# A planner's prices for transfers and GpSimd, and the order of the last seven products, in a two-layer encoder trunk

## The chip, the cores and the metric

The program runs on one core of one Trainium2 chip. The metric is the time of one execution on the device in microseconds; the median of several runs counts. The engines of a core run their own instruction queues in order and wait for each other by semaphores: TensorE (PE, matmuls), VectorE (DVE), ScalarE (ACT), GpSimd (POOL) and SyncE (SP, which here only issues transfers).

## The reference

Two layers over 1024 tokens of width 1024. The mixers (a convolution with a recurrence in layer 0, differential attention in layer 1) are not touched by the change; the feed-forward and the normalization behind it are:

```python
def layer_norm(x, g, b):
    mu = jnp.mean(x, axis=-1, keepdims=True)
    var = jnp.mean(jnp.square(x - mu), axis=-1, keepdims=True)
    return (x - mu) * lax.rsqrt(var + LN_EPS) * g + b

def swiglu(x, w_gate, w_up, w_down):
    return (jax.nn.silu(x @ w_gate) * (x @ w_up)) @ w_down

def reference(x, ...):
    for layer in range(DEPTH):
        y = conv_lru_mixer(x, ...) if layer % 2 == 0 else diff_attention_mixer(x, ...)
        x = layer_norm(DN_ALPHA * x + y, mix_ln_g[layer], mix_ln_b[layer])
        x = layer_norm(DN_ALPHA * x + swiglu(x, ffn_w_gate[layer], ffn_w_up[layer], ffn_w_down[layer]),
                       ffn_ln_g[layer], ffn_ln_b[layer])
    return x
```

D_FF is 2816, everything is float32.

## The kernel before

**Numbers and matmuls.** Each operand of a matmul is split into a high part (a cast to fp32r on ScalarE) and a low part (operand minus high part on VectorE): `split`. `three` then issues three matmuls, high by high, high by low and low by high, of 128x512 each.

**Stages.** Layer 0's input part runs from 0 to about 480 us, its feed-forward's gate and up part to 740 us, its down projection to 1000 us. Layer 1 with the attention follows to 1780 us, then its gate and up part to 2045 us and its down projection to the end. The activations of the feed-forward are 22 pages of 128x1024 (4 KB for each partition). 18 of them go out to memory (`a_d`); the last four stay on the chip.

**The down projection** (`ffn_down`) is a 2x2 block product with seven block products, M1 to M7, in place of eight. A block product sums over 11 columns f; for each f, `operands` makes a left operand out of stored activations and a right operand out of `in_down`, and four token tiles of three matmuls each are run on them: 7 x 11 x 12 = 924 matmuls of a layer. `plan` gives for each product what its operands are made of. `(0, 1), (1, 1), S` means that the block of half 1 of page f less the block of half 1 of page f + 11 is taken. A left sum runs on GpSimd. A right sum with A is two transfers: SyncE loads the first half, GpSimd issues a transfer that adds the second onto it in place. A right difference with S is two loads and a subtraction on VectorE. M3 and M4 have no left sum; M2 and M5 have no right sum. The products run in the order M3 M2 M5 M4 M1 M7 M6 and alternate between two sets of four PSUM banks, `al` and `be`. `into` adds a finished product into the residual pages `self.r` on VectorE (r11 and r12 are the left and right halves of token tiles 0 to 3, r21 and r22 those of tiles 4 to 7).

**Buffers.** `halloc` hands out half pages, of which five pages (ten halves) serve as `raws` and for left sums, in turn. `pair` hands out operand pages: first those lent from the transposed input `xt` (`lend`: eight for each token half), then pages of the general pool. `reclaim` ends the lending; before, it does so for both halves ahead of M6.

**The end of the down projection.** After M7 the tiles 0 to 3 are complete, and `done` normalizes them (`layer_norm`: two statistics, their aggregate and two passes of 1024 on VectorE, a power on GpSimd on a single column). M6 follows; its last three columns are run tile by tile, so that tiles 4 to 7 come one after the other, each with its own normalization. `late` loads gains, transposes tiles 0 to 3 for layer 1, or prefetches its weights.

**What sets the order.** All instructions are recorded (`note`) with a price (`price`), and `solve` plans them. It takes the engine whose next instruction can start first, and among the ready ones that with the earliest due time `late`, which is worked back from the order of TensorE. `apply` fixes the order so found for each engine. Prices and latencies of transfers therefore change where every instruction stands, in the whole program.

## Time and profile before

| | us |
|---|---|
| median of three runs | 2331.08 (2328.5 to 2335.04) |
| the profiled execution | 2323.4 |
| its span | 2321.6 |
| TensorE busy in it | 2168.9 |
| VectorE busy | 1862.2 |
| GpSimd busy | 1020.6 |
| ScalarE busy | 998.6 |

Times of the rows below are microseconds from the start of the span, unless they are marked ns. "g" is a page of the general pool, "xt" a page of the transposed input or one lent from it, "SM" the tile of small columns, "PS" PSUM. All instructions carry line L379 (L380 in the changed kernel), since a recorder issues them; tiles and shapes tell them apart. In the views that list waits, the engine behind the arrow ended the idle time.

### The profile page before, as it was taken

How to read it: one execution, taken by the hardware profiler on the slowest of the kernel's cores; microseconds unless marked ns; L12 is line 12 of the kernel's file. 1: busy time of each engine (PE TensorE's matmuls, PEld its weight loads, DVE VectorE, ACT ScalarE, POOL GpSimd, SP SyncE). 2: the span in 40 equal slices, each digit the busy share in tenths (PEclk: the TensorE clock that was granted, in tenths of full speed). 3: DMA queues.
4: the chain of work that ended last, by engine and by line, in shares of the span. 5: the costliest groups of instructions: out<-in, count | busy, mean ns of one | idle time of the engine just before them, and what ended most of it. 6: DMA issues, size and time to landing. Idle time of an engine off the chain costs nothing.

```text
span 2321.6 us, 28973 instructions
## 1 busy us (share of the span) xinstructions
PE 2168.9 (93%) x9856; PEld 1776.4 (77%) x9856; DVE 1862.2 (80%) x2735; ACT 998.6 (43%) x1751; POOL 1020.6 (44%) x798
## 2 busy tenths in 40 slices
PE   9999898899999999899999998979998999999995
PEld 7877676778888788678777776767776888888884
DVE  8988889887776589894788768767878877779888
ACT  6485336233333343332444445544544333334431
POOL 2123211186666455621334324222244776755464
PEclk9999999999999999999999998999999999999998
DMA  8348875464445866756455479575647444475684
GB/s 238 89 128 200 242 220 186 128 217 164 163 154 162 277 168 161 167 177 197 146 142 167 143 230 266 157 193 157 185 126 245 168 149 160 163 236 203 179 180 127
DMA packets 170084, 415.55 MB, mean 179 GB/s; under 512 B 18512, under 2 KB 38736, under 8 KB 169936
## 3 DMA queue, kind: packets, MB, share of 16 engines
q1 hardware_dynamic: 142864, 364.47, 48.3%
q0 software_dynamic: 27072, 49.24, 13.0%
q8 instruction: 78, 1.28, 0.2%
q14 instruction: 70, 0.57, 0.1%
HBM read 313.03 MB, written 85.98 MB: 172 GB/s over the span
## 4 chain that ended last, share of the span: by engine, by line
PE 65%; DMA 15%; DVE 12%; issue 4%; ACT 2%; POOL 2%; SPq 1%; DVEq 0%; ACTq 0%; POOLq 0%
PE PS L379 65%; DVE g L379 7%; DMA g<-in_down 4%; DMA g<-in_up 4%; DVE xt L379 3%; DMA g<-k_d 2%; ACT g L379 2%; DVE SM L379 2%; POOL g L379 1%; DMA g<-x_d 1%; DMA z_d<-g 1%; DMA g<-in_wout 1%; DMA k_d<-g 1%; SPq L379 1%; DMA q_d<-g 0%
## 5 line engine op out<-in xcount | busy, mean ns | idle before, releaser
L379 POOL TENSOR_TENSOR g<-g,g 128x512 f32<-128x512 f32 x390 | 621.2, 1605 | 509.8 <-ACT g L379 245.1
L379 PE MATMUL PS<-g,xt 128*128 128x512 f32 (+1 forms) x2800 | 646.8, 379 | 18.2 <-DVE g L379 11.0
L379 PE MATMUL PS<-xt,g 128*128 128x512 f32 x2428 | 614.1, 401 | 36.0 <-ACT g L379 19.6
L379 PE MATMUL PS<-xt 128*128 128x512 f32 (+1 forms) x2320 | 619.4, 393 | 10.5 <-ACT g L379 4.1
L379 PEld LDWEIGHTS PS<-g,xt 128*128 128x128 f32 x2800 | 516.1, 190 | 125.7 <-DVE g L379 14.3
L379 PEld LDWEIGHTS PS<-xt,g 128*128 128x128 f32 x2428 | 459.2, 192 | 145.2 <-ACT g L379 29.8
L379 DVE TENSOR_TENSOR xt<-g,xt 128x512 fp32r<-128x512 f32 x531 | 501.0, 969 | 76.4 <-ACT xt L379 73.9
L379 ACT CAST xt<-g 128x512 fp32r<-128x512 f32 x531 | 313.7, 619 | 510.6 <-PE PS L379 338.0
L379 DVE TENSOR_TENSOR g<-g,g 128x512 f32<-128x512 f32 (+2 forms) x457 | 444.5, 986 | 104.9 <-ACT g L379 78.6
L379 PEld LDWEIGHTS PS<-xt 128*128 128x128 f32 x2320 | 437.5, 190 | 105.9 <-ACT g L379 6.7
L379 DVE TENSOR_TENSOR g<-PS,g 128x512 f32<-128x512 f32 (+3 forms) x408 | 257.3, 643 | 159.7 <-PE PS L379 93.8
L379 ACT CAST g<-g 128x512 fp32r<-128x512 f32 (+1 forms) x248 | 188.0, 770 | 293.2 <-DVE g L379 73.6
L379 PE MATMUL PS<-g,g 128*128 128x512 f32 (+3 forms) x984 | 257.0, 381 | 31.1 <-DVE g L379 10.9
L379 DVE SCALAR_TENSOR_TENSOR g<-g,SM,g 128x512 f32<-128x512 f32 (+20 forms) x309 | 262.2, 883 | 2.5 <-POOL SM L379 0.5
L379 ACT ACTIVATE g<-PS,SM 128x512 f32<-128x512 f32 (+8 forms) x266 | 179.2, 688 | 136.6 <-PE PS L379 89.7
L379 PEld LDWEIGHTS PS<-g,g 128*128 128x128 f32 x984 | 176.6, 194 | 68.4 <-DVE g L379 13.7
L379 PE MATMUL PS<-xt,xt 128*128 128x512 f32 (+1 forms) x612 | 213.1, 391 | 1.3 <-DVE g L379 1.3
L379 POOL TENSOR_TENSOR g<-g 128x512 f32<-128x512 f32 x96 | 147.1, 1559 | 136.6 <-DMA g<-in_gate 95.0
L379 PE MATMUL PS<-SM,g 128*128 128x128 f32 (+1 forms) x704 | 113.4, 288 | 35.7 <-DVE g L379 23.0
L379 POOL TENSOR_TENSOR SM<-SM 128x1 f32<-128x1 f32 x96 | 80.7, 865 | 146.4 <-DVE SM L379 146.2
L379 PEld LDWEIGHTS PS<-SM,g 128*128 128x128 f32 x704 | 94.7, 164 | 53.9 <-DVE g L379 24.5
L379 PEld LDWEIGHTS PS<-xt,xt 128*128 128x128 f32 x612 | 115.1, 189 | 24.7 <-DVE g L379 1.7
(47 smaller groups left out, 1093.8 us busy)
## 6 DMA issues: line engine op xcount, KB each, us to landing
g<-in_up SPq DMA_DIRECT2D x88, 512.0 KB, 4.7
g<-in_down SPq DMA_DIRECT2D x176, 256.0 KB, 3.2
z_d<-g SPq DMA_DIRECT2D x44, 512.0 KB, 5.3
g<-in_gate SPq DMA_DIRECT2D x44, 512.0 KB, 4.2
g<-z_d SPq DMA_DIRECT2D x44, 512.0 KB, 4.1
g<-in_down POOLq DMA_DIRECT2D x88, 256.0 KB, 5.9
a_d<-g SPq DMA_DIRECT2D x36, 512.0 KB, 4.2
g<-a_d SPq DMA_DIRECT2D x36, 512.0 KB, 6.5
```

The costliest lines, as they stand in the source:

```text
L379: r = f(*a, **k)
```

## The change

The change does five things:

- Prices: GpSimd's sum of n columns goes from 2.106 n + 147 to 2.7 n + 150 ns, its `tensor_scalar` from 0.7 n + 300 to 0.9 n + 280 ns, its operations on up to 4 columns from 464 and 162 to 1000 and 700 ns. A transfer's latency in `solve` goes from 1000 + 1500 to 900 + 2000 ns (GpSimd) and from 650 to 1600 ns behind the issue (SyncE), on top of its bytes.
- The seven products run in the order M4 M5 M1 M7 M3 M2 M6. Tiles 0 to 3 are complete after M3, and are normalized in the program text after M2. The residual is read in column halves, one behind M4 and one behind M5.
- The left sums of M2 and M6 run on VectorE, not GpSimd.
- Tiles 0 to 3 are normalized by `layer_norm_act`: mean, variance and scaling on ScalarE, one pass on VectorE, and the shift `b` added by a transfer that GpSimd issues. This holds for both layers' feed-forward.
- The last six columns of M6, not three, are run tile by tile (`LAST`). `reclaim` ends the lending of token half 0 alone ahead of M6, so that M6 uses the lent pages of half 1.

The number of matmuls, 9790 instructions on TensorE, stays. GpSimd has 44 sums fewer and 8 transfers more; VectorE has 44 sums more, and 16 statistics, 8 aggregates and 8 passes fewer; ScalarE has 24 passes more.

```diff
             if n <= 4:
-                return 464.0 if name == "tensor_tensor" else 162.0, None
-            return (2.106 * n + 147 if name == "tensor_tensor" else 0.7 * n + 300 if name == "tensor_scalar" else n + 60), None
+                return 1000.0 if name == "tensor_tensor" else 700.0, None
+            return (2.7 * n + 150 if name == "tensor_tensor" else 0.9 * n + 280 if name == "tensor_scalar" else n + 60), None
...
                 if e == "pool":
-                    free[e] = s + 1000
-                    b = free[e] + 1500
+                    free[e] = s + 900
+                    b = free[e] + 2000
                 else:
                     free[e] = s + 60
                     hw = max(hw, s + 25) + 450
-                    b = hw + 650
+                    b = hw + 1600
...
+    def layer_norm_act(self, r, g, b, store=None):
+        nc = self.nc
+        mv = self.ring("mv", 4, 4)
+        j = self.alloc()
+        nc.scalar.activation(self.pg(j), r, AF.Identity, scale=-1.0 / D, accum_out=mv[:, 0:1])
+        nc.scalar.activation(self.pg(j), r, AF.Square, bias=mv[:, 0:1], accum_out=mv[:, 1:2])
+        self.release(j)
+        nc.vector.tensor_scalar(mv[:, 2:3], mv[:, 1:2], 1.0 / D, EPS, ALU.mult, ALU.add)
+        nc.gpsimd.tensor_tensor(mv[:, 3:4], mv[:, 2:3], self.mhalf, ALU.pow)
+        nc.vector.scalar_tensor_tensor(r, r, mv[:, 0:1], self.pg(g), ALU.add, ALU.mult)
+        nc.scalar.activation(r, r, AF.Identity, scale=mv[:, 3:4])
+        nc.gpsimd.dma_start(r, self.pg(b), accum_op=ALU.add)
+        if store:
+            store(slice(0, D))
...
-                nc.gpsimd.tensor_tensor(self.pg(s), src, act(f + n * ls[1][0], ls[1][1]), lop)
+                eng = nc.vector if m in (2, 6) else nc.gpsimd
+                eng.tensor_tensor(self.pg(s), src, act(f + n * ls[1][0], ls[1][1]), lop)
...
-        steps(3, al, range(n))
+        steps(4, al, range(n))
         for t in range(8):
             self.r[t] = self.alloc()
-            nc.sync.dma_start(self.pg(self.r[t]), self.x_d[t])
+        residual(0)
...
+        into(al, (r11, A), (r21, A))
+        steps(5, be, range(n))
+        residual(1)
+        into(be, (r11, S), (r12, A))
+        steps(1, al, range(n))
+        into(al, (r11, A), (r22, A))
+        steps(7, be, range(n))
+        into(be, (r11, A))
+        steps(3, al, range(n))
         into(al, (r12, A), (r22, A))
-        steps(2, be, range(n))
+        steps(2, be, range(3))
+        late(0)
+        steps(2, be, range(3, n))
+        for t in range(4):
+            done(t)
         into(be, (r21, A), (r22, S))
-        steps(5, al, range(n))
...
-        steps(7, be, range(n))
-        self.reclaim()
-        late(0)
-        for t in range(4):
-            nc.vector.tensor_tensor(r11[t], r11[t], be[t].ap, A)
-            self.unbank(be[t])
-            done(t)
-        get = lambda: self.alloc(True)
-        steps(6, al, range(5), get)
+        for t in be:
+            self.unbank(t)
+        self.reclaim(0)
+        steps(6, al, range(n - LAST))
         late(1)
-        steps(6, al, range(5, n - 3), get)
-        last = [operands(6, f, get) for f in range(n - 3, n)]
+        last = [operands(6, f, self.pair) for f in range(n - LAST, n)]
         late(2)
         for t in range(4):
             for i, (left, right) in enumerate(last):
-                step(al, left, right, t, False, i == 2)
+                step(al, left, right, t, False, i == LAST - 1)
             nc.vector.tensor_tensor(r22[t], r22[t], al[t].ap, A)
             self.unbank(al[t])
             done(t + 4)
...
         def done(t):
-            self.layer_norm(self.pg(self.r[t]), *self.gb)
+            (self.layer_norm_act if t < 4 else self.layer_norm)(self.pg(self.r[t]), *self.gb)
```

On GpSimd in M6 of layer 1, before; a DMA row is the issue of an accumulating load of a right operand, a sum with one input page is a left operand:

```order
L379 DMA g24_816_12860<-in_down 128x512
L379 TENSOR_TENSOR g2_810_12803<-g29_920_15199 128x512
L379 DMA g8_817_12878<-in_down 128x512
L379 TENSOR_TENSOR g8_817_12878<-g4_924_15279 128x512
L379 DMA g16_818_12886<-in_down 128x512
L379 TENSOR_TENSOR g23_815_12850<-g11_921_15219 128x512
L379 TENSOR_TENSOR g24_816_12860<-g13_922_15239 128x512
L379 DMA g23_815_12850<-in_down 128x512
```

The same stretch of GpSimd's queue in the changed kernel; g8_912, g21_913, g19_914 and g20_915 are the token tiles 0 to 3, g23_932 holds the shift:

```order
L380 DMA g9_804_12880<-in_down 128x512
L380 DMA g15_801_12844<-in_down 128x512
L380 DMA g28_796_12797<-in_down 128x512
L380 TENSOR_TENSOR SM_72<-SM_72 128x1 x2
L380 DMA g33_802_12854<-in_down 128x512
L380 TENSOR_TENSOR SM_72<-SM_72 128x1 x2
L380 DMA g8_912_15381<-g23_932_16344 128x1024
L380 DMA g21_913_15382<-g23_932_16344 128x1024
L380 DMA g19_914_15383<-g23_932_16344 128x1024
L380 DMA g20_915_15384<-g23_932_16344 128x1024
L380 DMA g2_803_12872<-in_down 128x512
L380 DMA g9_804_12880<-in_down 128x512
```

The sums of M6 have left this queue, and the four additions of the shift stand behind five of M6's eleven accumulating loads and ahead of the other six.

On VectorE in M6 of layer 1, before; pages g5, g15 to g30 and g14, g21 with numbers of 930 to 937 are token tiles, the subtractions into pages numbered 956 to 963 are low parts of the last operands:

```order
L379 TENSOR_TENSOR g6_956_16617<-g16_818_12886,g6_956_16617 128x512
L379 TENSOR_TENSOR g26_957_16635<-g8_817_12878,g26_957_16635 128x512
L379 BN_AGGR SM_72<-SM_72 128x2
L379 TENSOR_SCALAR SM_72<-SM_72 128x1
L379 BN_STATS SM_72<-g15_934_15403 128x6
L379 BN_STATS SM_72<-g30_935_15405 128x6
L379 TENSOR_TENSOR g10_959_16656<-g16_818_12886,g10_959_16656 128x512
L379 TENSOR_TENSOR g28_960_16659<-g2_810_12803,g28_960_16659 128x512
L379 BN_STATS SM_72<-g14_936_15407 128x6
L379 SCALAR_TENSOR_TENSOR g0_930_15395<-g0_930_15395,SM_72,g33_945_16488 128x1024
L379 TENSOR_TENSOR g7_962_16680<-g23_815_12850,g7_962_16680 128x512
L379 TENSOR_TENSOR g12_963_16698<-g2_810_12803,g12_963_16698 128x512
```

In the changed kernel the one pass for each of tiles 0 to 3 stands behind M6's fifth left sum (one page in, a raw half out), ahead of its sixth:

```order
L380 TENSOR_TENSOR g9_804_12880<-g22_924_15488 128x512
L380 TENSOR_SCALAR SM_72<-SM_72 128x1
L380 SCALAR_TENSOR_TENSOR g8_912_15381<-g8_912_15381,SM_72,g27_931_16342 128x1024
L380 TENSOR_SCALAR SM_72<-SM_72 128x1
L380 SCALAR_TENSOR_TENSOR g21_913_15382<-g21_913_15382,SM_72,g27_931_16342 128x1024
L380 TENSOR_SCALAR SM_72<-SM_72 128x1
L380 SCALAR_TENSOR_TENSOR g19_914_15383<-g19_914_15383,SM_72,g27_931_16342 128x1024
L380 TENSOR_SCALAR SM_72<-SM_72 128x1
L380 SCALAR_TENSOR_TENSOR g20_915_15384<-g20_915_15384,SM_72,g27_931_16342 128x1024
L380 TENSOR_TENSOR xt0_74<-g2_803_12872,xt0_74 128x512 x2
L380 TENSOR_TENSOR g2_803_12872<-g5_925_15508 128x512
L380 TENSOR_TENSOR xt0_74<-g9_804_12880,xt0_74 128x512
```

The statistics of tiles 0 to 3 are gone from VectorE, and the one pass a tile that is left stands earlier: among the operands of M6's middle columns and ahead of the sums of M2's banks, where before it stood among the last operands of M6.

## Rows read from the trace of the kernel before

**Rows 1.** The page: busy time of each engine, chain that ended last.

```profile
PE 2168.9 (93%) x9856; PEld 1776.4 (77%) x9856; DVE 1862.2 (80%) x2735; ACT 998.6 (43%) x1751; POOL 1020.6 (44%) x798
...
PE 65%; DMA 15%; DVE 12%; issue 4%; ACT 2%; POOL 2%; SPq 1%; DVEq 0%; ACTq 0%; POOLq 0%
```

**Rows 2.** By stage: length, busy PE, PEld, DVE, ACT, POOL; clock, DMA, GB/s.

```profile
0.00:480.00 480.00, 437.50 (x1882) 349.50 (x1883) 423.95 (x651) 256.20 (x381) 117.53 (x119) 0.97 0.67 183
480.00:780.00 300.00, 300.00 (x1324) 248.11 (x1322) 216.78 (x267) 104.71 (x177) 197.11 (x131) 1.00 0.52 172
780.00:820.00 40.00, 35.56 (x145) 27.52 (x144) 25.49 (x31) 18.07 (x32) 20.54 (x16) 0.96 0.75 259
...
960.00:1000.00 40.00, 26.02 (x109) 20.14 (x109) 34.52 (x47) 11.85 (x21) 22.31 (x19) 0.83 0.59 129
1000.00:1780.00 780.00, 713.19 (x3519) 589.62 (x3518) 595.06 (x1060) 358.32 (x709) 243.15 (x212) 0.95 0.62 179
...
2100.00:2260.00 160.00, 159.31 (x702) 131.29 (x701) 142.06 (x170) 66.14 (x118) 95.93 (x76) 1.00 0.67 172
2260.00:2303.00 43.00, 37.11 (x156) 29.80 (x154) 36.46 (x51) 8.71 (x15) 19.62 (x17) 0.92 0.58 135
```

**Rows 3.** The same view, 20 us at the start in layer 0.

```profile
780.00:800.00 20.00, 16.76 (x65) 12.67 (x64) 9.39 (x15) 6.42 (x11) 7.16 (x7) 0.91 1.04 395
```

**Rows 4.** Timeline of TensorE, last product of layer 0, then of layer 1.

```profile
977.10 1.22 PE L379 MATMUL PS<-g,g 128*128 128x512 f32 x2 [6.91 <-ACT g L379]
...
2265.18 11.04 PE L379 MATMUL PS<-g,g 128*128 128x512 f32 x48
...
2282.84 20.38 PE L379 MATMUL PS<-g,g 128*128 128x512 f32 x82 [5.05 <-DVE g L379]
```

**Rows 5.** The chain in order of time, layer 1's end: start, us, what.

```profile
2223.76 7.24 DMA g<-in_down
...
2233.38 5.52 DMA g<-in_down
```

**Rows 6.** DMA issues of the down projection: count, KB, median us to landing.

```profile
g<-in_down SPq DMA_DIRECT2D x176, 256.0 KB, 3.2
...
g<-in_down POOLq DMA_DIRECT2D x88, 256.0 KB, 5.9
```

**Rows 7.** GpSimd by shape (busy, mean); issue of a transfer (min/median/max ns).

```profile
L379 POOL TENSOR_TENSOR g<-g 128x512 f32<-128x512 f32 x96 | 147.1, 1559 | 136.6 <-DMA g<-in_gate 95.0 <-DVE xt L379 15.9 <-DVE g L379 9.5
...
L379 POOL TENSOR_TENSOR SM<-SM 128x1 f32<-128x1 f32 x96 | 80.7, 865 | 146.4 <-DVE SM L379 146.2
...
L379 POOL DMA_DIRECT2D g<-in_down x88: 856/882/1882, 739.0 to 2286.5; - x88
```

**Rows 8.** VectorE by shape: 2040-2070 us, then 2240-2265 us (two rows).

```profile
L379 DVE TENSOR_TENSOR xt<-g,xt 128x512 fp32r<-128x512 f32 x11 | 8.2, 744 | 1.1 <-ACT xt L379 1.1
...
L379 DVE TENSOR_TENSOR xt<-g,xt 128x512 fp32r<-128x512 f32 x10 | 13.4, 1382 | 0.0
...
L379 DVE TENSOR_TENSOR g<-g,PS 128x512 f32<-128x512 f32 x8 | 5.1, 675 | 0.0
```

**Rows 9.** VectorE and ScalarE by shape, whole span.

```profile
L379 DVE SCALAR_TENSOR_TENSOR g<-g,SM,g 128x1024 f32<-128x1024 f32 x67 | 86.0, 1311 | 0.8 <-POOL SM L379 0.5
...
L379 DVE BATCH_NORM_STATS2 SM<-g 128x6 f32<-128x512 f32 x64 | 42.2, 684 | 1.1 <-POOL g L379 0.5
...
L379 DVE TENSOR_TENSOR g<-g 128x512 f32<-128x512 f32 x45 | 35.2, 786 | 10.1 <-POOL g L379 8.8 <-DMA g<-in_down 1.1
...
L379 ACT ACTIVATE g<-g,SM 128x1024 f32<-128x1024 f32 x4 | 4.7, 1163 | 5.0 <-POOL SM L379 4.7 <-DVE SM L379 0.3
```

**Rows 10.** Timeline of VectorE, then GpSimd, after the last matmuls.

```profile
2302.77 0.21 DVE L379 BATCH_NORM_AGGREGATE SM<-SM 128x2 f32<-128x12 f32 x1
...
2311.22 6.19 DVE L379 SCALAR_TENSOR_TENSOR g<-g,SM,g 128x1024 f32<-128x1024 f32 x6
...
2303.31 1.45 POOL L379 TENSOR_TENSOR SM<-SM 128x1 f32<-128x1 f32 x1 [6.28 <-DVE SM L379]
```

More of the change, by code (lines that the diff above doesn't have):

```diff
@@ L27 @@
 HALO = 32
+LAST = 6
 NTAP = 8
@@ L446, in setup @@
         self.ring_x = deque()
-        self.lent = False
+        self.lent = set()
         self.banks = deque(range(8))
@@ L491, in lend @@
     def lend(self, h):
-        self.lent = True
+        self.lent.add(h)
         for i in range(8):
             t = (self.XTH, self.XTL)[i // 4][:, 2 * (i % 4):2 * (i % 4) + 2, h * HALF:(h + 1) * HALF]
-            self.ring_x.append(Page(t, True, "x", i))
+            self.ring_x.append(Page(t, True, "x", 8 * h + i))
     def trim(self, want):
@@ L507, in trim, with reclaim @@
                     self.free.append(i)
-    def reclaim(self):
-        self.lent = False
-        self.ring_x.clear()
+    def reclaim(self, *halves):
+        for h in halves or (0, 1):
+            self.lent.discard(h)
+        self.ring_x = deque(p for p in self.ring_x if p.kind != "x" or p.idx // 8 in self.lent)
     def release(self, *pages):
@@ L517, in release @@
             elif p.kind == "x":
-                if self.lent:
+                if p.idx // 8 in self.lent:
                     self.ring_x.append(p)
@@ L1321, in step, with steps @@
                        self.part(right, 1), start, stop)
-        def steps(m, banks, fs, get=self.pair):
+        def steps(m, banks, fs):
             for f in fs:
-                left, right = operands(m, f, get)
+                left, right = operands(m, f, self.pair)
                 for t in range(4):
@@ L1328, in steps @@
                 self.release(left, right)
-                if m == 7:
+                if m == 2:
                     self.release(acts.pop(f + n))
@@ L1340, in into, with residual @@
                     nc.vector.tensor_tensor(r[t], r[t], banks[t].ap, op)
-        steps(3, al, range(n))
+        def residual(h):
+            for t in range(8):
+                cs = slice(h * HALF, (h + 1) * HALF)
+                nc.sync.dma_start(self.pg(self.r[t])[:, cs], self.x_d[t][:, cs])
+        steps(4, al, range(n))
         for t in range(8):
             self.r[t] = self.alloc()
-            nc.sync.dma_start(self.pg(self.r[t]), self.x_d[t])
+        residual(0)
         r11, r12 = [[self.pg(self.r[t])[:, h * HALF:(h + 1) * HALF] for t in range(4)] for h in range(2)]
         r21, r22 = [[self.pg(self.r[t + 4])[:, h * HALF:(h + 1) * HALF] for t in range(4)] for h in range(2)]
-        into(al, (r12, A), (r22, A))
-        steps(2, be, range(n))
-        into(be, (r21, A), (r22, S))
-        steps(5, al, range(n))
-        into(al, (r12, A), (r11, S))
-        steps(4, be, range(n))
-        into(be, (r21, A), (r11, A))
-        steps(1, al, range(n))
-        into(al, (r22, A), (r11, A))
-        steps(7, be, range(n))
-        self.reclaim()
-        late(0)
-        for t in range(4):
-            nc.vector.tensor_tensor(r11[t], r11[t], be[t].ap, A)
-            self.unbank(be[t])
-            done(t)
-        get = lambda: self.alloc(True)
-        steps(6, al, range(5), get)
+        into(al, (r11, A), (r21, A))
[7 more added lines that the diff above has]
+        steps(3, al, range(n))
+        into(al, (r12, A), (r22, A))
+        steps(2, be, range(3))
[3 more added lines that the diff above has]
+            done(t)
+        into(be, (r21, A), (r22, S))
+        for t in be:
+            self.unbank(t)
+        self.reclaim(0)
+        steps(6, al, range(n - LAST))
         late(1)
-        steps(6, al, range(5, n - 3), get)
-        last = [operands(6, f, get) for f in range(n - 3, n)]
+        last = [operands(6, f, self.pair) for f in range(n - LAST, n)]
         late(2)
@@ L1377, in ffn_down @@
             self.release(left, right)
+        self.reclaim()
         self.release(*acts.values())
@@ L1829, in store @@
                 nc.sync.dma_start(io["out"][0][t * P:(t + 1) * P, cs], self.pg(self.r[t])[:, cs])
-            self.layer_norm(self.pg(self.r[t]), *self.gb, store=store, parts=2 if t == 7 else 1)
+            if t < 4:
+                self.layer_norm_act(self.pg(self.r[t]), *self.gb, store=store)
+            else:
+                self.layer_norm(self.pg(self.r[t]), *self.gb, store=store, parts=2 if t == 7 else 1)
         self.cap = 8
```

## The prediction

> **What bounds the kernel now.** I read the busy table first: TensorE is busy 2168.9 us of a span of 2321.6 us, so 152.7 us of the span are its idle time, and the chain that ended last runs 65% over TensorE, 15% over transfers and 12% over VectorE [rows 1]. So the kernel is bound by TensorE, and a change can only give back time in which it idles, or in which its clock is below full. Next I cut the span into stages [rows 2]. In the middle of a feed-forward (480 to 780 us) TensorE never idles; 1324 matmuls in 300 us are 226.6 ns each, my price of a matmul. The lost time lies in five places: the input layer (480 - 437.5 = 42.5 us idle), the attention layer (780 - 713.2 = 66.8 us idle), the start of the down projection of layer 0 (780 to 820 us), its end (960 to 1000 us), and the end of layer 1 from 2260 us. The change rebuilds the last three and reorders the first two.
>
> The start: 145 matmuls in 40 us need 145 x 0.2266 = 32.9 us, so 7.1 us are lost, while the 16 transfer engines are all full (share 1.04, 395 GB/s in 780 to 800 us) [rows 2, 3]. The end of layer 0: 109 matmuls in 40 us need at most 24.7 us, so 15.3 us or more are lost, of which 14.0 us are idle time; the mean granted clock of these 40 us is 0.83, between its levels of 1.2 and 2.4 GHz, and 6.91 us of the idle time came in one piece [rows 2, 4]. The end of layer 1: the last product, 132 matmuls, runs from 2265.18 to 2303.22 us, 38.0 us where 132 x 0.2266 = 29.9 us are needed; 8.1 us are lost, 5.05 us of them in one idle piece [rows 4]. After its last matmul another 18.4 us pass to 2321.6 us, and in them VectorE works and TensorE doesn't.
>
> Why the last product starves is to be seen in the chain there: a load of `in_down` of 7.24 us, then GpSimd, then one of 5.52 us [rows 5]. Each right operand of M7 and M6 is two transfers in series (SyncE, median 3.2 us; GpSimd, 5.9 us [rows 6]), and GpSimd, which issues the second, has a 1.56 us sum for the left operand before it [rows 7]. VectorE, which makes the low parts, is held back: the same 128x512 subtraction takes 744 ns at 2040 to 2070 us and 1382 ns at 2240 to 2265 us, while its sums with one input from PSUM take 675 ns in that stretch [rows 8]. And the first four rows of tiles are normalized in the same 38 us, eight passes of VectorE of 1.31 us [rows 9].
>
> **Part 1: the order of products and the engine of the left sums.** Removed from GpSimd: 22 sums a layer x 1.559 us = 34.3 us [rows 7]. Added to VectorE: 22 x 0.786 us, its own row for that shape, = 17.3 us [rows 9]. M2, which has no accumulated operand, now comes just ahead of M6, so GpSimd's queue is nearly empty when M6's transfers are due, and the operands of M6 can be prepared ahead while M2 runs. The raw halves are still ten (five pages) and M6 takes two for each of its 11 columns, so five columns are in flight, 5 x 12 x 0.2266 = 13.6 us of TensorE; the way round is 3.2 + 5.9 us of transfers plus 1.5 us for cast and subtraction (an estimate: twice the 0.744 us of the faster subtraction, rows 8), 10.6 us, and 1 us of hops. That fits with 2 us to spare, where the sums on GpSimd and a blocked VectorE (1.38 us) had used that up. The bounds for what is given back: nothing, when the ring stays the limit, and all of 15.3 and 8.1 us. I take most of both, 11 us in layer 0 and 6 us in layer 1, since three causes are taken away at once.
>
> **Part 2: the start.** Before, the first product needs 11 stored activations of 512 KB and 22 loads of 256 KB, 11.0 MB in 30 us. M4 needs activations 11 to 21, of which four never left the chip: 7 x 0.5 + 5.5 = 9.0 MB. The residual `x_d` is read in two halves, one after M4 and one after M5, not 4 MB at once. A stretch at 395 GB/s gets a fifth less to move. Between 0 and 7.1 us; I take 3. Layer 1 loses 160 - 702 x 0.2266 = 0.9 us from 2100 to 2260 us [rows 2], and I give it nothing.
>
> **Part 3: four normalizations on ScalarE.** Removed from VectorE for each tile: two statistics (0.684 us each), one aggregate (0.21 us), one pass (1.311 us) [rows 9, 10], 2.9 us, or 11.5 us a layer. With the 17.3 us of part 1 VectorE has 5.8 us more a layer, if nothing blocks it. Added on ScalarE: three passes of 1024, by the nearest row 1.163 us each [rows 9], 3.5 us a tile, 14.0 us a layer. ScalarE is busy 8.7 of 43 us there [rows 2], so this is hidden. Added on GpSimd: four accumulating transfers of 512 KB; the issue costs 0.882 us (median, up to 1.882 us) [rows 7], 3.5 us a layer against 34.3 us removed. What stands behind them in its queue are the last six accumulating loads of M6. Their data comes by the time TensorE has done the first five columns, so I price this at nothing; if the cover is gone, see the second rival.
>
> **Part 4: the tail.** LAST goes from 3 to 6, so the last four tiles come from TensorE at 18 x 0.2266 = 4.1 us apart, not 2.0 us. A tile costs VectorE 0.68 (sum) + 0.68 (second statistic) + 0.21 + 2 x 1.31 = 4.2 us [rows 8 to 10], so it now keeps pace, falling 0.1 us behind at each of three tiles. After the last matmul there remain one tile (0.68 + 0.68 + 0.21 + 1.31 us, and half of the second pass, 0.66 us, since the last tile is stored in halves), the power on GpSimd (1.45 us where it waits), some 2 us of hops between engines (an estimate, from the 1.45 us that one such step took), and the 4.2 us that pass from VectorE's last instruction (2317.4 us) to the end [rows 10]: 11.2 us in place of 18.4 us. 7 us; I take 6, bounds 3 and 8.
>
> **Part 5: the planner's prices.** The new prices are nearer to the rows. A GpSimd sum of 512 columns is planned at 1532 ns, not 1225 ns (row: 1559); the single-element power at 1000 ns, not 464 ns (row: 865); a 256 KB load at 2.8 us, not 1.9 us (row: 3.2), an accumulating one at 3.6 us, not 3.2 us (row: 5.9) [rows 6, 7]. So consumers of transfers are queued later, and engines stand less at the head of their queue for data that isn't there. That matters in the 109 us of idle time of the input and attention layers. But the accumulating transfers are still planned too short, and VectorE, which is busy 595 of 780 us there [rows 2], gets another order altogether. It can go either way; a tenth of the idle time is 11 us, and I take 2 us of gain with bounds of 12 us to both sides.
>
> **Sum:** 11 + 6 + 3 + 6 + 2 = 28 us. The profiled execution took 2323.4 us (its span and 1.8 us around it), so it would take 2295 us; it lay 7.7 us under the median of the runs, 2331.1 us, against which the forecast is made: 2303 us.
>
> Against part 3 speaks a rule of the Trainium skill (SBUF — State Buffer, SBUF: two separate sides): GpSimd writes the descriptors of the transfers it issues, and VectorE's two-port operations lock it out meanwhile. The change adds four such transfers to VectorE's busiest stretch. By the rows the issue never took more than 1.0 us over its median [rows 7], so by that rule at most 4 us a layer of the 28 us would go, 20 us being left.
>
> **The rivals.** First, VectorE becomes the bound of the end. In M3, M2 and M6 (90 us of TensorE) it has 66 subtractions x 0.744 us = 49.1 us, 22 sums x 0.786 us = 17.3 us, 24 sums from PSUM x 0.675 us = 16.2 us and 8 us of passes and statistics of normalizations, 91 us in all; that is full, less what it did ahead in M7. If a third of the subtractions still take 1.382 us [rows 8] (GpSimd still blocking), it needs 14 us more a layer, 105 us, and M6 starves as before. Then parts 1 and 5 give nothing and 9 us are left: 2322 us. For it: VectorE is busy 142 of 160 us before the end of layer 1 [rows 2]. Against: GpSimd has no more sums in these three products.
>
> Second, slower: GpSimd's queue is held by the four transfers of part 3. They wait for ScalarE's scaling, that for the power on GpSimd, that for VectorE, that for ScalarE's second pass. Four tiles are 14.0 us of ScalarE, whose queue also holds casts that wait for `in_down`. If the normalizations aren't done when TensorE is through the first five columns of M6, six accumulating loads stand behind them, and TensorE waits up to 14.0 + 5.9 us a layer. It decides from the point where ScalarE's passes begin later than about 13.6 us before that. Half of it in both layers, 20 us, on top of the old losses of M6 and less 9 us of parts 2 and 4: 2342 us.
>
> Third, the ends improve, and the new order of the input and attention layers costs what they give: VectorE's order there is rearranged in many places, and a quarter more idle time is 27 us: 2330 us.
>
> **How the numbers follow.** A measurement can tell 0.3%, 7 us, from no change: faster is below 2324 us, slower above 2338 us. Forecast 0.60 (2289 to 2318 us), first rival 0.13 (two thirds of it faster), second 0.14 (slower), third 0.13 (a quarter faster, the rest the same but for 0.02 slower). Faster: 0.60 + 0.08 + 0.03 = 0.71; same: 0.05 + 0.08 = 0.13; slower: 0.14 + 0.02 = 0.16. The range, 2284 to 2338 us, leaves out 0.16 above and about 0.04 below.
>
> **What would show it.** In the profile after: the last product of layer 1 in 30 to 33 us; no idle time of TensorE over 2 us in the end of layer 0, at full clock; under 13 us from the last matmul to the end; 145 or more matmuls in the 40 us at the start; subtractions near 0.7 us in the last two products. It is wrong if the accumulating loads of M6 wait behind transfers of 128x1024 on GpSimd, if VectorE has no idle time in M2 and M6 and TensorE waits for it, or if the idle time of the attention layer grows by more than 10 us.

## The result

| | before | changed |
|---|---|---|
| median of the runs, us | 2329.8 (2324.9 to 2335.0) | 2272.6 (2269.9 to 2273.0) |
| ratio, 95% interval | | 0.9768 (0.9739 to 0.9797) |
| span of the profiled execution, us | 2321.6 | 2270.6 |
| mean granted clock of TensorE | 0.970 | 0.979 |

The changed kernel is faster by 57 us in the medians and by 51 us in the profiled spans. The sign is the forecast one; the gain is about twice the forecast 28 us, and the time lies below the range. The page of the changed kernel, busy time of each engine and then the chain that ended last (before: [rows 1]):

```profile
PE 2151.8 (95%) x9856; PEld 1769.1 (78%) x9856; DVE 1852.9 (82%) x2747; ACT 1025.0 (45%) x1791; POOL 980.8 (43%) x762
...
PE 66%; DMA 16%; DVE 9%; issue 4%; ACT 3%; POOL 1%; SPq 1%; DVEq 0%; POOLq 0%; ACTq 0%
```

TensorE's idle time fell from 152.7 to 118.8 us, and the same matmuls took 17.1 us less busy time: the granted clock was at its lower level, 1.2 GHz, for some 98 us of the span, where it had been there for 140 us. By stage, with the columns of [rows 2] (length, busy PE, PEld, DVE, ACT, POOL; clock, DMA, GB/s):

```profile
780.00:820.00 40.00, 39.65 (x175) 32.53 (x174) 28.50 (x32) 15.82 (x28) 22.24 (x16) 1.00 0.69 225
...
960.00:1000.00 40.00, 31.10 (x138) 24.99 (x137) 34.19 (x50) 12.61 (x22) 12.63 (x11) 0.87 0.33 69
1000.00:1755.00 755.00, 698.92 (x3523) 581.74 (x3523) 581.61 (x1045) 363.16 (x721) 253.48 (x218) 0.97 0.66 190
```

The attention layer, 3519 matmuls in 780 us before, now does 3523 in 755 us: the largest single piece of the gain is where the forecast had put 2 us. Stages of two kernels don't lie at the same microseconds, so the table cuts every profile at the same number of matmuls (interpolated in windows of 10 us, so that a figure is good to about 2 us). It gives us of the stage, and TensorE's idle time in brackets where it matters. The columns behind the change are runs that are told below.

| stage (matmuls) | before | change | its prices alone | its end alone | change, tiles 0 to 3 on VectorE |
|---|---|---|---|---|---|
| input layer, operands (0 to 1800) | 460.2 | 456.8 | 456.1 | 462.2 | 457.3 |
| start of down, layer 0 (3100 to 3400) | 75.7 (4.4) | 68.6 (0.4) | 68.3 | 72.2 | 69.3 |
| M6, layer 0 (3900 to 4230) | 89.3 (14.0) | 81.7 (8.9) | 90.0 (14.0) | 79.6 (5.9) | 76.7 (4.4) |
| attention layer (4230 to 7700) | 770.8 (66.9) | 746.4 (56.1) | 739.2 (48.9) | 778.8 (78.3) | 739.1 (48.1) |
| M6, layer 1 (9680 to 9840) | 44.3 (5.9) | 43.5 (3.5) | 42.7 | 45.9 | 37.6 (0.3) |
| from matmul 9840 to the end | 22.1 | 14.1 | 21.0 | 13.4 | 16.0 |
| span | 2321.6 | 2270.6 | 2278.1 | 2312.9 | 2254.6 |

The stages left out differ by about 2 us at most between these five. The change, profiled on a second chip, took 740.1 us in the attention layer, so a difference of some 6 us there says little.

### The profile page after: what moved, and what is told of

It is laid out like the page before. It is cut to its first block, busy times and chain, and to the rows that moved or that the text cites. A ratio compares the mean times of both kernels' runs of the same rounds, so it can differ in the third digit from the quotient of the medians.

```text
span 2270.6 us, 28995 instructions
## 1 busy us (share of the span) xinstructions
PE 2151.8 (95%) x9856; PEld 1769.1 (78%) x9856; DVE 1852.9 (82%) x2747; ACT 1025.0 (45%) x1791; POOL 980.8 (43%) x762
## 4 chain that ended last, share of the span: by engine, by line
PE 66%; DMA 16%; DVE 9%; issue 4%; ACT 3%; POOL 1%; SPq 1%; DVEq 0%; POOLq 0%; ACTq 0%
PE PS L380 66%; DVE g L380 6%; DMA g<-in_down 5%; DMA g<-in_up 4%; ACT g L380 2%; DMA g<-g 2%; DVE xt L380 2%; DMA z_d<-g 1%; DMA g<-k_d 1%; DVE SM L380 1%; POOL g L380 1%; DMA g<-a_d 1%; DMA g<-in_wout 1%; SPq L380 1%; DMA k_d<-g 1%
## 5 line engine op out<-in xcount | busy, mean ns | idle before, releaser
L380 POOL TENSOR_TENSOR g<-g,g 128x512 f32<-128x512 f32 (+1 forms) x368 | 601.1, 1645 | 518.2 <-DVE g L380 243.9
L380 PE MATMUL PS<-xt 128*128 128x512 f32 x2536 | 668.9, 392 | 15.3 <-ACT xt L380 6.6
L380 PE MATMUL PS<-xt,g 128*128 128x512 f32 x2428 | 612.6, 401 | 37.6 <-ACT g L380 23.5
L380 PEld LDWEIGHTS PS<-g,xt 128*128 128x128 f32 x2800 | 516.2, 190 | 118.4 <-ACT g L380 11.1
L380 PEld LDWEIGHTS PS<-xt 128*128 128x128 f32 x2536 | 475.9, 189 | 117.0 <-ACT xt L380 8.4
L380 ACT CAST xt<-g 128x512 fp32r<-128x512 f32 x567 | 334.5, 619 | 513.0 <-PE PS L380 330.8
L380 ACT CAST g<-g 128x512 fp32r<-128x512 f32 (+1 forms) x212 | 167.2, 796 | 200.1 <-DVE g L380 67.2
L380 PE MATMUL PS<-g,g 128*128 128x512 f32 (+3 forms) x768 | 197.2, 367 | 13.8 <-ACT g L380 7.8
L380 PEld LDWEIGHTS PS<-g,g 128*128 128x128 f32 x768 | 132.6, 190 | 40.0 <-ACT g L380 10.3
L380 POOL DMA_DIRECT2D g<-in_down x88 | 84.4, 1053 | 169.8 <-DMA g<-in_down 161.4
L380 POOL DMA_DIRECT2D g<-g x64 | 60.1, 1023 | 192.7 <-ACT g L380 131.8
L380 POOL TENSOR_TENSOR g<-g 128x512 f32<-128x512 f32 x74 | 114.0, 1581 | 63.1 <-DMA g<-in_gate 33.0
```

The lines of the kernel that those rows point to most:

```text
L380: r = f(*a, **k)
```

## The experiments

Each run is given as the ratio of its time to that of the kernel before in the same session (95% interval).

**Which half of the change brings the gain?** The kernel before with all the new prices, and the change with the old ones:

> The kernel before with the new prices alone (GpSimd's operations and both latencies), products in the old order. Theory A, the prices act mainly in the input and attention layers and account for the part of the gain that the end of the feed-forward doesn't: 24 to 34 us below before, about 2300 us, with the idle time of the attention layer down by some 12 us. Theory B, the gain in the attention layer comes with the new end of layer 0 (other buffers and other timing at its start): within 8 us of before.

> The change with the old prices: products in the new order, left sums of M2 and M6 on VectorE, four normalizations on ScalarE, last six columns tile by tile. Theory A: the ends give 22 to 32 us, about 2302 us, and the attention layer is as long as before. Theory B: nearly all of the gain is here, 2275 to 2285 us.

Prices alone 0.9811 (0.9794 to 0.9828); the new end alone 0.9954 (0.9931 to 0.9977). The two gains add up to 0.9765, the change's own 0.9768. So the prices are worth 44 us in the medians (2278.2 against 2322.1), three or four times the end (13 us). That is more than either theory gave the prices, and less than either gave the end. In the table they give 31.6 us in the attention layer, 4 us in the input layer and 7.4 us at the start of the down projection. The last had been put down to fewer bytes, but with the old order of products, and so the old bytes, it is all there; the new order alone gives 3.5 us of it.

**Which prices?** The kernel before with the new prices of GpSimd's computing alone, and with the new latencies of transfers alone:

```diff
 # new prices of GpSimd's computing alone
-                return 464.0 if name == "tensor_tensor" else 162.0, None
+                return 1000.0 if name == "tensor_tensor" else 700.0, None
...
 # new latencies alone
...
-                    b = free[e] + 1500
+                    b = free[e] + 2000
...
-                    b = hw + 650
+                    b = hw + 1600
```

> The kernel before with GpSimd's new compute prices alone. Theory A1, the latencies of transfers are what counts: within 8 us of before. Theory A2, GpSimd's prices count (a sum was planned a fifth too short): most of what the run with all prices gains, over 15 us.

> The kernel before with the new latencies of transfers alone. Theory A1: most of what the run with all prices gains, over 15 us, and fewer waits of TensorE for k_d in the attention layer. Theory A2: within 8 us of before.

GpSimd's prices alone: 0.9996 (0.9980 to 1.0012), nothing. The latencies alone: 0.9890 (0.9866 to 0.9914). Both together are 0.9811, so GpSimd's prices bring 17 us once the latencies are right, and nothing before. The place is in the second half of the attention layer (matmuls 6200 to 7200). TensorE's waits there, before, with the latencies and with all prices (us in total, times, longest):

```profile
PE PS L379 <- DVE g L379: 19.1, 8, 7.3
```

```profile
PE PS L379 <- DVE SM L379: 7.2, 3, 5.8
PE PS L379 <- DVE g L379: 6.7, 6, 1.5
```

```profile
PE PS L379 <- ACT g L379: 4.6, 3, 3.1
PE PS L379 <- DVE g L379: 4.0, 5, 1.3
```

This stretch takes 214.7 us before, 214.9 us with GpSimd's prices alone, 207.1 us with the latencies, 195.9 us with both. The long single waits for VectorE go one after the other. With GpSimd's prices alone the wait for `DVE g` fell as well (to 11.1 us), but that for ScalarE grew from 6.0 to 10.3 us.

**Is it the accuracy of SyncE's latency, or luck of another order?** The change with 1100 and 2400 ns in place of 1600, and, as a control, with a constant of the planner that is no price at all:

```diff
-                    b = hw + 1600
+                    b = hw + 1100
...
-                    b = hw + 1600
+                    b = hw + 2400
...
-    patience = 1500
+    patience = 1400
```

> The change with SyncE's transfers planned at 1100 ns in place of 1600 ns, halfway back to the 650 ns of before. Theory A: about half of the gain of the latencies goes, 8 to 18 us slower than the change, in the attention layer above all. Theory C: within a scatter of 10 us of the change.

> The change with SyncE's transfers planned at a latency of 2400 ns in place of 1600 ns (a 512 KB load at 4.3 us; the profile after has 4.2 to 4.5 us, the plan of the change 3.5 us). Theory A: as fast as the change or 2 to 8 us faster, the stretch from the attention layer's middle again shorter. Theory C: a scatter of 10 us to either side.

> The change with the planner's constant patience at 1400, not 1500: it stands for nothing that the chip does, and only reorders some instructions. It gives the scatter that reordering alone brings. Theory A: within 5 us of the change in the whole and in each stretch. Theory C: 8 to 15 us to one side, in the attention layer above all.

1100 ns: 0.9865 (0.9825 to 0.9905), 2400 ns: 0.9768 (0.9721 to 0.9814), the control: 0.9798 (0.9764 to 0.9831). So half the correction loses some 20 us of the gain (11 us in the profiled spans), more than 1600 gives nothing further that these runs can tell, and the control moves the time within the intervals. The control is a small one: compared place by place in its queue, VectorE has another operation or other pages than in the change at 95 of 2747 places, with 1100 ns at 295. The other runs of this document are a wider one, since each of them orders the program anew. Cut at the matmuls themselves, the attention layer (4230 to 7700) takes:

| SyncE's latency, ns | profiles | attention layer, us | its first half (4700 to 5600), us |
|---|---|---|---|
| 650 | 3 | 765.9 to 780.1 | 196.9 to 200.1 |
| 1100 | 1 | 753.6 | 194.0 |
| 1600 | 12 | 736.7 to 752.1 | 185.2 to 192.5 |
| 2400 | 2 | 732.8 and 737.5 | 184.7 and 185.5 |

The 752.1 us are the run with GpSimd's old prices; the other eleven at 1600 ns, whatever their order, lie within 9 us (736.7 to 745.4). So the prices set the time, and not the luck of one order. The first half of the attention (matmuls 4700 to 5600) shows the mechanism. With the columns of the stages above, the kernel before (650 ns), then 1100, 1600 and 2400 ns:

```profile
1138.50:1338.90 200.40, 187.52 (x904) 156.17 (x903) 163.70 (x314) 90.72 (x196) 77.59 (x63) 0.97 0.53 155
```

```profile
1122.80:1316.50 193.70, 183.88 (x901) 152.75 (x899) 161.41 (x312) 90.59 (x195) 78.05 (x63) 0.98 0.56 163
```

```profile
1117.50:1304.40 186.90, 180.28 (x902) 150.74 (x901) 159.13 (x308) 90.38 (x195) 78.92 (x62) 1.00 0.58 168
```

```profile
1122.80:1307.30 184.50, 180.51 (x901) 150.47 (x899) 158.64 (x312) 90.42 (x195) 80.25 (x62) 1.00 0.59 175
```

And TensorE's wait for loads of `k_d` in the same four stretches:

```profile
PE PS L379 <- DMA g<-k_d: 5.7, 4, 2.1
```

```profile
PE PS L380 <- DMA g<-k_d: 6.9, 4, 2.7
```

```profile
PE PS L380 <- DMA g<-k_d: 1.5, 2, 0.8
```

```profile
PE PS L380 <- DMA g<-k_d: 0.2, 1, 0.2
```

The longer a load is planned, the shorter the stretch: 200.4, 193.7, 186.9, 184.5 us. The last three kernels differ in this constant alone. The kernel before lacks the other edits too, and its waits for `k_d` are shorter than those at 1100 ns. Of the 13.5 us from before to the change, 6.3 us are idle time (12.9 to 6.6 us), 4.2 of them waits for `k_d`. The other 7.2 us are busy time of the same matmuls. In the kernel before the granted clock was at its lower level twice in this stretch, for 6.8 us each (clock in the third column from the end):

```profile
1193.80:1200.60 6.80, 5.98 (x20) 5.21 (x21) 4.28 (x10) 4.10 (x9) 2.76 (x4) 0.50 0.32 94
1268.90:1275.70 6.80, 6.28 (x21) 5.45 (x22) 3.33 (x8) 1.93 (x7) 2.46 (x4) 0.50 0.26 81
```

Both times it fell during the second of two waits that lay close together: 0.75 and 1.91 us for `k_d`, then 1.27 us (no cause shown) and 2.06 us for `k_d`. In the changed kernel it never fell in this stretch. So a wait removed was paid twice here: 13.6 us at half the clock cost up to 6.8 us. None of these constants is the truth. A load of `k_d` lands 6.1 us after its issue in the kernel before (number, KB, median us), where the planner has 1.9 us at 650 ns, 2.8 us at 1600 ns and 3.6 us at 2400 ns, apart from what it counts for transfers ahead:

```profile
g<-k_d SPq DMA_DIRECT2D x64, 256.0 KB, 6.1
```

Over the whole attention layer the waits for `k_d` are the smaller part of what went: with the prices alone they fell from 11.0 to 6.7 us, of 66.9 us of idle time that became 48.9. Most of it were waits for VectorE, before and with the prices alone; those for pages of ScalarE grew from 11.5 to 18.9 us:

```profile
PE PS L379 <- DVE g L379: 35.5, 19, 7.3
```

```profile
PE PS L379 <- DVE g L379: 16.4, 13, 4.2
```

**Is a price nearer to the trace always better?** An accumulating load of GpSimd takes 6.7 us in the changed kernel. Planned longer:

```diff
-                    b = free[e] + 2000
+                    b = free[e] + 4500
```

> The change with GpSimd's transfers planned at 900 + 4500 ns in place of 900 + 2000 ns, which puts an accumulating load of 256 KB at 6.1 us (the profile after has 6.7 us, the plan of the change 3.6 us). Theory A, accuracy counts: the stretches that wait for accumulating loads, 0 to 480 us and the end of layer 1, get 4 to 12 us shorter in sum. Theory C, what counts is that any reordering came out well this time: between 15 us shorter and 15 us longer, without relation to these stretches.

0.9879 (0.9843 to 0.9915): some 25 us slower than the change by the ratios, 14 us in the profiled spans, which neither theory had. M6 gains in both layers (76.3 and 36.5 us), but TensorE now waits in M1 and M7, which it didn't before: 123.6 us in place of 113.1 us for matmuls 3400 to 3900, and 98.2 in place of 85.9 us in the same place of layer 1. TensorE there, and the chain:

```profile
866.05 5.75 PE L380 MATMUL PS<-xt 128*128 128x512 f32 x24 [1.15 <-DVE xt L380]
875.49 32.79 PE L380 MATMUL PS<-xt 128*128 128x512 f32 x131 [3.68 <-DVE xt L380]
```

```profile
871.24 4.94 DMA g<-in_down
...
879.15 8.62 DMA g<-in_down
```

So no: the truer price lets something else run first, and a load of the ring of ten raw halves comes late. Which instruction was preferred to it wasn't settled.

**What did the new end give, part by part?** The old order of products in the change; the left sums of M2 and M6 back on GpSimd; the tiles 0 to 3 normalized by VectorE as before; and LAST = 3:

```diff
 # the first product, and so on, as before: M3 M2 M5 M4 M1 M7 M6
-        steps(4, al, range(n))
+        steps(3, al, range(n))
...
-                eng = nc.vector if m in (2, 6) else nc.gpsimd
+                eng = nc.gpsimd
...
-            (self.layer_norm_act if t < 4 else self.layer_norm)(self.pg(self.r[t]), *self.gb)
+            self.layer_norm(self.pg(self.r[t]), *self.gb)
...
-LAST = 6
+LAST = 3
```

> The change with the products in the old order M3 M2 M5 M4 M1 M7 M6, tiles 0 to 3 normalized behind M7; prices, left sums of M2 and M6 on VectorE, normalization on ScalarE and six last columns as in the change. If the order is what ends the starving of M6: 8 to 16 us longer than the change, mostly at the end of layer 0 (idle time of 10 us or more there). If the other edits do: within 3 us.

> The change with the left sums of M2 and M6 back on GpSimd. The prediction's part 1 (the sums' way off GpSimd is one of three causes of the starving last product): 6 to 12 us longer than the change, with the last product of layer 1 over 33 us. Rival: the order of the products and the normalization alone make the end, within 3 us of the change, a ratio to before of 0.976 to 0.978.

> The change with the four normalizations back on VectorE (in the place after M3 and M2). If VectorE is short in M2 and M6, 4 to 10 us longer than the change; if the normalization is early enough to hide in M2 on either engine, within 3 us of it.

> The change with three, not six, last columns tile by tile. The prediction's part 4: the tail after the last matmul of layer 1 is 6 us longer (17 to 18 us, where the change has about 10 us), the whole 5 to 7 us longer. Rival, tiles closer together end earlier and only VectorE's queue grows: within 2 us.

- Old order: 0.9749 (0.9717 to 0.9782), no slower than the change; M6 takes 81.3 us (as the change) and 37.9 us, 5.6 us less. The order of products is not what helps; in layer 1 it even costs, for a reason that is told below.
- Left sums on GpSimd: 0.9829 (0.9797 to 0.9861); M6 85.4 and 48.9 us, 3.7 and 5.4 us more than in the change. VectorE's subtraction is at 1014 ns in M6 of layer 1, in the change at 684 ns. VectorE by shape, changed kernel (2175 to 2235 us), then with the sums on GpSimd (2185 to 2240 us):

```profile
L380 DVE TENSOR_TENSOR xt<-g,xt 128x512 fp32r<-128x512 f32 x42 | 26.9, 684 | 4.6 <-ACT xt L380 4.6
L380 DVE TENSOR_TENSOR g<-g,PS 128x512 f32<-128x512 f32 x17 | 10.8, 680 | 0.0
```

```profile
L380 DVE TENSOR_TENSOR xt<-g,xt 128x512 fp32r<-128x512 f32 x32 | 30.8, 1014 | 5.2 <-ACT xt L380 5.2
```

- Tiles 0 to 3 on VectorE: 0.9731 (0.9702 to 0.9759), no slower than the change, where the expectation had it up to 10 us slower, and M6 takes 76.7 and 37.6 us, 5.0 and 5.9 us less; the tail takes 1.9 us more. So the normalization on ScalarE, priced at nothing, cost about 11 us of M6's gain in this order of products and with six last columns.
- LAST = 3: 0.9785 (0.9757 to 0.9813), not to be told from the change. The tail costs 4.1 us more (14.4 us behind the last matmul, in the change 10.4 us) and M6 takes 4.9 and 6.0 us less: the six columns bring two thirds of the forecast 6 us in the tail, and M6 pays for them, since their operands must all be there at once, and they come late. The same 11 us of M6 go by this edit and by the one before, so they are the price of the two together, the normalization on ScalarE and six last columns.

**Where does the normalization on ScalarE cost?** The changed kernel's transfers between 2213 and 2232 us, first the queues (share of all 16 engines), then the issues with KB and median us to landing:

```profile
q0 software_dynamic: 864, 2.62, 76.1%
...
g<-g POOLq DMA_DIRECT2D x4, 512.0 KB, 8.6
out_x<-g SPq DMA_DIRECT2D x4, 512.0 KB, 11.4
g<-in_down SPq DMA_DIRECT2D x5, 256.0 KB, 9.8
g<-in_down POOLq DMA_DIRECT2D x3, 256.0 KB, 9.3
```

The four accumulating transfers of the shift (2.1 of the 2.62 MB of GpSimd's queue) fill the engines, and a load of SyncE, 3.6 us in the median of the program, takes 9.8 us here. SyncE's queue, changed kernel and then with the tiles on VectorE:

```profile
2220.01 1.31 SPq L380 DMA_DIRECT2D out_x<-g  x1
2221.52 1.25 SPq L380 DMA_DIRECT2D g<-in_down  x1
2222.86 6.74 SPq L380 DMA_DIRECT2D out_x<-g  x3
2229.70 4.18 SPq L380 DMA_DIRECT2D g<-in_down  x2
```

```profile
2181.30 38.78 SPq L380 DMA_DIRECT2D g<-in_down  x12
2229.47 20.67 SPq L380 DMA_DIRECT2D out_x<-g  x8
```

In the change the stores of the finished tiles wait at the head of SyncE's queue for the shift to land (4.6 us in two waits), and one of M6's last three loads is issued behind the first store, two behind all four. On VectorE all twelve loads go first. TensorE's end in the changed kernel (for before, [rows 4]):

```profile
2240.27 1.31 PE L380 MATMUL PS<-xt 128*128 128x512 f32 x3 [1.49 <-ACT xt L380]
2242.98 2.88 PE L380 MATMUL PS<-xt 128*128 128x512 f32 x6 [1.40 <-ACT xt L380]
...
2258.70 1.55 PE L380 MATMUL PS<-g,g 128*128 128x512 f32 x6
```

The run with the old order keeps the normalization on ScalarE, but there the shift comes later. Its queues of SyncE, then of GpSimd:

```profile
2174.99 47.89 SPq L380 DMA_DIRECT2D g<-in_down  x17
2237.85 7.12 SPq L380 DMA_DIRECT2D out_x<-g  x3
```

```profile
2226.24 1.78 POOL L380 DMA_DIRECT2D g<-in_down  x2
...
2232.69 0.87 POOL L380 DMA_DIRECT2D g<-g  x1
```

All loads of M6 are issued before the first shift (2232.69 us) and the first store, and TensorE has no wait over the whole end, from 2190 us on. So it isn't the transfers as such that cost in layer 1, but where the new order of products puts them: ahead of M6's last loads, as the piece of GpSimd's queue in the section on the change shows. Late loads alone don't cost either. The run with LAST = 3 has the same four transfers and the same order in SyncE's queue:

```profile
2218.06 6.79 SPq L380 DMA_DIRECT2D out_x<-g  x3
2224.95 4.19 SPq L380 DMA_DIRECT2D g<-in_down  x2
```

Yet TensorE waits 0.8 us in that end, where it waits 3.4 us in the change.

Layer 0 has no such stores; there the transfers meet M6's loads directly: from 935 to 966 us the same four take 13.0 us in the median, and M6's loads 9.2 us (SyncE) and 7.6 us (GpSimd). TensorE waits:

```profile
971.95 2.32 PE L380 MATMUL PS<-SM,g 128*128 128x128 f32 x8 [6.19 <-DVE xt L380]
976.89 1.97 PE L380 MATMUL PS<-SM,g 128*128 128x128 f32 x8 [2.62 <-DVE xt L380]
```

These matmuls are transposes of the finished tiles for layer 1. They wait for VectorE to empty a PSUM bank, VectorE comes to that behind an operand of M6 for which it has waited 4.23 us, and ScalarE's cast for it waits for an accumulating load that was issued at 951.36 us, behind the shift, and landed at 965.09 us:

```profile
965.19 1.14 ACT L380 CAST xt<-g 128x512 fp32r<-128x512 f32 x2 [10.33 <-DMA g<-in_down]
```

With the tiles on VectorE 4.4 us of these 8.8 us of waits are left. In the run with the old order the transposes wait for the shift itself, 7.8 us of 9.7 us of waits there:

```profile
967.50 0.69 PE L380 MATMUL PS<-SM,g 128*128 128x128 f32 x2 [7.04 <-DMA g<-g]
```

The shift added by GpSimd itself, in place of the transfer:

```diff
-        nc.gpsimd.dma_start(r, self.pg(b), accum_op=ALU.add)
+        nc.gpsimd.tensor_tensor(r, r, self.pg(b), ALU.add)
```

> The change with the shift of the four normalizations added by GpSimd's tensor_tensor of 1024 columns instead of by an accumulating transfer. If the four transfers of 512 KB slow the loads of M6: the last product of layer 1 and the end of layer 0 are shorter, 5 to 12 us in all, as with the normalization on VectorE. If ScalarE's passes delay the casts: within 3 us of the change.

0.9793 (0.9760 to 0.9827), no better than the change. M6 of layer 1 falls from 43.5 to 40.6 us, that of layer 0 rises from 81.7 to 87.5 us. There GpSimd's sums of 1024 stand beside VectorE's subtractions, three of which took 5.91, 3.43 and 3.64 us. VectorE by shape between 936 and 975 us, changed kernel and then this run:

```profile
L380 DVE TENSOR_TENSOR xt<-g,xt 128x512 fp32r<-128x512 f32 x16 | 11.6, 769 | 5.1 <-ACT xt L380 5.1
```

```profile
L380 DVE TENSOR_TENSOR xt<-g,xt 128x512 fp32r<-128x512 f32 x14 | 19.9, 1463 | 0.9 <-ACT xt L380 0.9
```

TensorE's longest wait in that M6, 3.06 us, ended with the last of the three. So this run trades one cost for another and doesn't tell in layer 0 what the transfers alone are worth. In layer 1 some 3 of the 5.9 us come back without them; the stores of the tiles still stand ahead of the last loads in this kernel's queue of SyncE.

**Is there a better kernel?** On one chip: the change again, with the tiles on VectorE and 2400 ns, and with the tiles on VectorE and the old order of products:

> The change itself again, as the yardstick on the chip of the other three of this call: 0.974 to 0.980 of before.

> Normalizations on VectorE, as in the run that was faster than the change, and SyncE's transfers planned at 2400 ns. Theory A: both gains add, 10 to 18 us under the change, the middle of the attention layer near 184 us. Theory C: no nearer than 5 us to that.

> The products in the old order and the normalizations on VectorE, behind M7; new prices, left sums of M2 and M6 on VectorE, six last columns. If the old order is fast only because ScalarE took the normalization off VectorE there, M6 starves as it did before, 10 to 20 us over the change; if the left sums and the prices are what feeds M6, within 6 us of the run with the new order and the normalizations on VectorE.

The change 0.9775 (0.9745 to 0.9806), tiles on VectorE with 2400 ns 0.9724 (0.9691 to 0.9757), with the old order 0.9751 (0.9721 to 0.9781). The second is 9 us below the change in the medians (2257.9 against 2267.0), and though the intervals of the ratios overlap, all six runs of it (2246.0 to 2258.7 us) lie below all six of the change (2262.0 to 2271.1 us). The third pays for its M6 in the tail, 17.1 us behind the last matmul in place of 10.4 us. In both, M6 of layer 1 has lost all its idle time (36.5 and 36.1 us for 160 matmuls, which need 36.3 us).

## Why the prediction was off

- **The bound**: right. TensorE's idle time and clock are where all of the gain came from.
- **Part 5, the prices** (forecast 2 us, bounds 12 to both sides): this is the step that failed. Alone they give 44 us. The working took "a tenth of the idle time" with no row behind it, and it left out the clock: beside its 66.8 us of idle time the attention layer lost busy time, which [rows 2] show as a clock of 0.95. It also said that truer prices could go either way, "since VectorE gets another order altogether". In the runs another order at the same prices moves the attention layer by 9 us at most, where the prices alone move it by 31.6 us, and the latency of SyncE's loads, planned 1.3 us too short by the prediction's own numbers (1.9 us against 3.2 us, [rows 6]), was a real cause that could have been looked up in TensorE's waits for `k_d`. Most of the idle time that went were waits for VectorE (35.5 to 16.4 us), so VectorE's other order, which the working named as a risk, seems to have been part of the gain. That caution was right for one price alone, the accumulating loads (25 us slower when planned nearer to the trace).
- **Part 1** (11 and 6 us): measured 7.6 us in layer 0 and 0.8 us in layer 1. Of the three causes that it named, VectorE held back by GpSimd's sums was real: subtractions of 684 ns where it was 1382 ns for the ten of [rows 8], and 3.7 and 5.4 us lost when the sums go back. The order of products was none, and in layer 1 it moved the shift ahead of M6's last loads.
- **Part 3** (hidden): wrong, about 11 us in the two layers with the six last columns of part 4, and that is what was missing in part 1. The cover that it named, five columns of TensorE's work, was there for GpSimd's queue, but not for the transfer engines, which carry M6's operands too, and not for SyncE's queue, which the prediction didn't look at.
- **Part 2** (3 us): 7.1 us, 175 matmuls in the 40 us of [rows 2] where 145 had been, but the prices alone do it, so the reason was wrong.
- **Part 4** (6 us): right. From the last matmul (2260.25 us) to the end it is 10.4 us, where 11.2 us were worked out; the stage of the table gains 8.0 us. But LAST = 6 gives only 4.1 us of it; the rest is there with LAST = 3 too, so the number was met in part by luck. That M6 pays for it beside part 3 (LAST = 3) wasn't foreseen.
- By the profile the terms came to 8.4 + 7.1 + 8.0 us, and 27.8 us for the input and attention layers, together 51.3 us.

**The rivals.** The first fell: VectorE's subtractions are at 684 ns, the late operands wait for transfers, and with four more normalizations on VectorE M6 was shorter, not longer. The third fell in sign: the attention layer gained 24 us. The second had the right place and the wrong queue: GpSimd issued the four transfers of layer 1 in one go (3.56 us from 2214.84 us), so nothing was held up behind ScalarE; the delay came in the transfers themselves and in SyncE's queue, 11 us in place of 20. The rule of the Trainium skill on VectorE locking out GpSimd's descriptors (SBUF — State Buffer, SBUF: two separate sides) would have been seen in the issue times. Among M6's accumulating loads the longest took 1.94 us in layer 1 and 2.82 us in layer 0, against a median of 0.86 us, but these spans overlap the instruction before on GpSimd: counted from its end, no issue in the two ends took more than 0.90 us. The 1.0 us over the median that the prediction counted [rows 7] were such an overlap too (0.91 us at most by this count). So the issue times here show nothing of it.

**What stays open**: why GpSimd's prices help only on top of the latencies (the waits in the second half of the attention layer are shown, the decision of the planner behind them isn't); which instruction goes ahead of the late load when accumulating loads are planned at 4500 ns; and in layer 0 of the change itself, how much of M6's loss is the shift's transfers and how much the other loads beside them, since half of the waits stay when the shift goes.

## What to carry to other kernels

When a static plan orders the engines, compare each of its latencies with the trace first: transfers planned too short, SyncE's by about 1 us, cost 27 us, a rebuilt end of both layers brought 13 us. Test each price by itself all the same, since one that was truer made the kernel slower. A reordering should be tried several times at the same prices, to know what order alone does (9 us in the attention layer here). Work that is moved off a busy engine onto transfers isn't free when the same transfer engines carry the next operands, and a store that waits for it belongs behind the loads in its queue: look at where the moved work lands in each queue, not only at its sum.

## What was unexpected of the hardware

- Accumulating transfers of 512 KB from page to page, issued one behind the other, land one after the other: in layer 1 the first 4.81 us after its issue, the next three 3.0 to 3.3 us apart. The median of all eight from issue to landing, 11.0 us, is mostly that queue; those of 256 KB take 6.2 us in the median, 3.3 us at the least.
- VectorE's 128x512 subtraction takes 684 ns with no GpSimd sums of two inputs beside it, 1014 ns with those of M6, and 1382 ns before [rows 8]; beside GpSimd's sums of 1024 three took 3.4 to 5.9 us, while its sums with an input from PSUM stay at 675 to 680 ns.
- In the first half of the attention ten waits of TensorE of at most 2.4 us, 12.8 us in 200 us, came with a granted clock of 0.97; six of at most 2.0 us, 6.5 us in all, with 1.00. The same stretch of matmuls then took 180.3 in place of 187.5 us of busy time.
